# The first layer's start reordered: x first, modulation in two column halves

## The chip, the cores and the metric

One core of a Trainium2 chip runs the whole program in one launch. The metric is device time in microseconds (us), lower is better. TensorE (PE) multiplies and transposes, ScalarE (ACT), VectorE (DVE) and GpSimd (POOL) work on tiles, SyncE (SP) issues nearly all DMAs, in the order of its queue.

## The reference

The input x has 512 rows of 1024 columns. The program is a first block of four layers (gated linear attention "gla", a spatial gating unit, an attention with forget gates, and gla again) and a second block of two layers with a context stream. Only the start of the first layer is touched by the change:

```
cond = silu(c)                               # 1 x 1024
mod = cond @ w_mod[0] + b_mod[0]             # w_mod[0]: 1024 x 3072
shift, scale, gate = split(mod, 3)
h = rms_norm(x, norm_pre_g[0]) * (1 + scale) + shift
q, k, v, z, a_low = split(h @ gla_w_in[0])   # then decay, attention in chunks, head norm
o = (rms_norm(o, g_head) * silu(z)) @ w_out
x = x + gate * rms_norm(o, norm_post_g[0])
```

Shift and scale are one value for each of the 1024 columns of h. A product h @ W sums over these columns, in eight pieces of 128 (k = 0 to 7).

## The kernel before

Products are made from split operands: the left side H and each weight are held as a high part (fp32r) and the rest (low), and three products (hi·hi, hi·lo, lo·hi) are summed in PSUM. `weights` loads a weight tile ("wr", 256 KB, 5 buffers), and `split` writes "wh" on ScalarE and "wl" on GpSimd or DVE in turn (L256, L257; 4 buffers each). Large tiles of one row block (4 KB per partition) share the ring "t4" of 28 buffers. PSUM has eight banks, four for "pp" (products) and four for "pa" (the rest).

`setup` loads the identity, columns of c, `b_mod` and `norm_pre_g`, and makes `cond`. Then it loads the first 2048 columns of `w_mod[0]` in 16 tiles of 128 x 1024 (eight k, for each the shift and the scale columns), with the four tiles of x in the middle of them (`load_x` after the eighth). Each tile is multiplied with `cond`, in four column groups of 256 (L164). DVE copies the sums, TensorE transposes them, and DVE adds the bias and forms the multiplier, so that `m` (16 values for each of 128 partitions) holds the multiplier and the shift as columns (L166 to L183).

`first_block` begins with `prenorm`: x is normalized by row (`normed`: squares and a half on ScalarE, the rate on GpSimd, the other half on DVE), 32 transposes turn it (L501), and each transposed tile is read from PSUM with multiplier and shift (L507 on ScalarE, L509 on DVE) and split into H.hi and H.lo (L256, L257). All of this needs `m`. Then `gla` begins: the values of head 0 (`proj_tok`, K = 8, 256 columns, weights in four groups of two k; L310 to L312), `gla_decay` (L675 to L700), then q and k of head 0 (`proj_T`, L358 to L360), the attention, the gate z. The row `gh` (the head gains, broadcast over 128 partitions, 512 KB) is loaded as `gla` begins.

Generators yield at certain points; at each yield the driver takes 0.6 of a step (MRATE) of the background queue, which computes the modulations of the later layers (`mods`, L389 to L393). After the first group of the values (ADV = 1) `consts` loads the constants of the later stages. The Tile framework's planner turns the written program into the order of each engine's queue: it goes by priority (the order of writing) and by a simulated timeline, so each engine's queue is fixed when the kernel is built, and it need not be the order of writing.

Of the kernel before, what the change touches and what calls it, by code (L numbers as in the profile page):

```python
# [21 lines left out]
D = 1024  # L22
# [54 lines left out]
class Core:  # L77
    def __init__(self, ctx, tc, A):
        self.ctx, self.tc, self.nc, self.A = ctx, tc, tc.nc, A
        pool = lambda name, bufs, **k: ctx.enter_context(tc.tile_pool(name=name, bufs=bufs, **k))  # L80
        self.cp = pool("const", 1)
        self.wp = pool("w", 3)
        self.mx = pool("mx", 2)
        self.sm = pool("sm", 4)
        self.dp = pool("dram", 1, space=DRAM)
        self.ps = pool("ps", 1, space=PSUM)
        self.turn = {}
        self.n = 0
        self.ph, self.nlo = "", {}
        self.bg, self.rate, self.owed = {"m": [], "c": []}, {"m": MRATE, "c": 0}, {"m": 0, "c": 0}  # L90
        self.two = "c_2" in A
        self.share = False
        self.sk = ""

# [44 lines left out]
    def setup(self):  # L139
# [13 lines left out]
        w = [self.t("t4", [128, D]) for _ in range(16)]  # L153
        for i, x in enumerate(w):
            k, v = i // 2, i % 2
            nc.sync.dma_start(x, A["w_mod"][0][k * 128:(k + 1) * 128, v * D:(v + 1) * D])
            if i == 7:
                self.load_x()
        pad = self.cond["c"]
        ps = [self.psA() for _ in range(2)]  # L160
        for i, x in enumerate(w):
            k, v = i // 2, i % 2
            for g in range(4):
                nc.tensor.matmul(ps[v][g * 32:(g + 1) * 32, :256], pad[:, k, :], x[:, g * 256:(g + 1) * 256],  # L164
                                 start=(k == 0), stop=(k == 7))
        m = self.small("mcol", [128, 16], bufs=3)  # L166
        bias = self.col("b_mod0", 16)
        for v in (1, 0):
            sb = self.t("t1", [128, 256])
            nc.vector.tensor_copy(sb, ps[v][:, :256])  # L170
            pt = self.psA()
            for h in range(2):
                nc.tensor.transpose(pt[:, h * 128:(h + 1) * 128], sb[:, h * 128:(h + 1) * 128], self.ident)

            col = pt[:, :256].rearrange("p (h g r) -> p g h r", h=2, r=32)[:, :, :, 0]
            o = m[:, 8 - 8 * v:16 - 8 * v].rearrange("p (g h) -> p g h", h=2)
            bv = bias[:, v * 8:v * 8 + 8].rearrange("p (g h) -> p g h", h=2)
            nc.vector.tensor_tensor(o, col, bv, op=ALU.add)
            if v:
                pre = self.small("pre0", [128, 8], bufs=1)  # L180
                nc.vector.tensor_scalar(pre, self.col("pre0", 8), 32.0, None, ALU.mult)
                nc.vector.scalar_tensor_tensor(m[:, 0:8], m[:, 0:8], 1.0, pre, ALU.add, ALU.mult)
        self.m0 = m  # L183
# [104 lines left out]
    def proj_tok(self, H, nt, W, K, c0, n, out, r0=0, each=None, inturn=False, lead=1, wide="pp"):  # L288
# [42 lines left out]
        for g in groups:  # L331
            ws = [(k0, nk, self.weights(W, r0 + k0, nk, c0, n)) for k0, nk in g]
# [295 lines left out]
    def gla(self, H, j, O):  # L628
        nc, A = self.nc, self.A
        W = A["gla_w_in"][j]  # L630
        gh = self.bcast(A["gla_g_head"][j].rearrange("h d -> (h d)"), 1024, "t4")
        nc.vector.tensor_scalar(gh, gh, 0.5, None, ALU.mult)
# [9 lines left out]
        for h in range(4):  # L642
            v = []
            if h == 0:

                yield from values(h, v)
                yield from self.gla_decay(H, j, b)
            o = []
# [1523 lines left out]
    def first_block(self, dst=None):  # L2172
        A, x = self.A, self.x
        H, step = self.prenorm(x, 4, self.m0)
        for t, xn in enumerate([self.normed(x(t)) for t in range(4)]):
            step(t, xn)
        if ADV == 0:
            self.consts()
        yield
        for i in range(4):  # L2180
# [3 lines left out]
            if i % 3 == 0:  # L2184
                gen = self.phase("gla", self.gla(H, i // 3, O))
                if i == 0 and ADV:

                    for _ in range(ADV):
                        next(gen)
                        yield  # L2190
# [32 lines left out]
ADV = 1  # L2223
# [69 lines left out]
```

## Time and profile before

| | us |
|---|---|
| median of 3 runs | 3268.89 |
| lowest and highest run | 3267.01, 3275.14 |
| the profiled execution's own time | 3273.38 |
| its span | 3271.6 |
| TensorE busy in it | 3099.9 |
| DVE, ScalarE, GpSimd busy in it | 1691.7, 1458.9, 1306.4 |

The median is the time that a change is judged by. The profile is of one execution; its times begin at the span's start. An engine's busy time is what its instructions took, so what is missing to the span is idle time. A DMA share of 1.00 means that all 16 DMA engines are busy. Matmul records overlap (the array is pipelined), so the distance between two starts is the cost of one, not its printed duration. The clock column is the TensorE clock that was granted: 1.00 is 2.4 GHz, 0.50 is 1.2 GHz, and values between are means over a stretch that has both.

### The profile page before, as it was taken

What the parts mean: (1) busy time and instruction counts of PE and PEld (TensorE: products, weight loads), DVE (VectorE), ACT (ScalarE), POOL (GpSimd) and SP (SyncE); (2) the same over time, 40 slices, a digit from 0 to 9 for tenths busy, and PEclk for the clock granted to TensorE, in tenths of its full rate; (3) what the DMA queues carried; (4) which work ended last, traced back from release to release, by engine and by line L of the source; (5) the groups of instructions that cost most, each with busy time, mean ns of one, the idle gap of its engine ahead of it and who ended that gap; (6) DMA issues with size and microseconds to landing.
All of it is one profiled execution on the core that took longest, in us unless ns stands there. A gap on an engine that the chain in (4) does not pass through costs nothing.

```text
span 3271.6 us, 61127 instructions
## 1 busy us (share of the span) xinstructions
PE 3099.9 (95%) x23487; PEld 2650.2 (81%) x23487; DVE 1691.7 (52%) x3554; ACT 1458.9 (45%) x3173; POOL 1306.4 (40%) x1312
## 2 busy tenths in 40 slices
PE   7999999999999999989999999899999989999998
PEld 4878889878877778878887789898888877888887
DVE  2744564454555564666897757651112468641112
ACT  3424544354544543345544544453323447643323
POOL 2544453232212345344543113554445341154445
PEclk9999999999989999999999999999999999999999
DMA  7355645754435625354564335353333330043332
GB/s 239 91 152 171 212 132 165 235 164 133 134 117 169 191 76 150 113 160 128 164 171 130 109 86 144 114 160 94 100 123 110 109 90 2 24 142 97 97 123 90
DMA packets 477420, 426.25 MB, mean 130 GB/s; under 512 B 108038, under 2 KB 421609, under 8 KB 477129
## 3 DMA queue, kind: packets, MB, share of 16 engines
q1 hardware_dynamic: 477129, 422.35, 43.0%
q8 instruction: 185, 3.03, 0.4%
q14 instruction: 106, 0.87, 0.1%
HBM read 383.66 MB, written 38.03 MB: 129 GB/s over the span
## 4 chain that ended last, share of the span: by engine, by line
PE 74%; DVE 10%; DMA 5%; ACT 4%; issue 3%; POOL 3%; SPq 1%; POOLq 0%; DVEq 0%; ACTq 0%
PE ffn.pp L359 6%; PE ffn.pp L358 6%; PE ffn.pp L360 6%; PE mods.pa L393 3%; PE out.pp L310 2%; PE out.pp L311 2%; PE out.pp L312 2%; PE ffn.pa L312 2%; PE ffn.pa L311 2%; PE ffn.pa L310 2%; DMA mods.wm<-in_w_mod_dram 2%; PE fox.pp L312 1%; PE fox.pp L311 1%; PE fox.pp L310 1%; PE sgu.pp L310 1%
## 5 line engine op out<-in xcount | busy, mean ns | idle before, releaser
L257 POOL TENSOR_TENSOR ffn.wl<-ffn.wr,ffn.wh 128x512 fp32r<-128x512 f32 x258 | 332.8, 1293 | 345.6 <-ACT ffn.wh L256 345.5
L256 ACT ACTIVATE ffn.wh<-ffn.wr 128x512 fp32r<-128x512 f32 x258 | 162.5, 631 | 348.3 <-PE ffn.pp L360 144.6
L358 PE MATMUL ffn.pp<-pre.t,ffn.wh 128*128 128x512 f32 x672 | 261.6, 389 | 0.0
L359 PE MATMUL ffn.pp<-pre.t,ffn.wl 128*128 128x512 f32 x672 | 261.4, 389 | 0.0
L360 PE MATMUL ffn.pp<-pre.t,ffn.wh 128*128 128x512 f32 x672 | 261.4, 389 | 0.0
L598 DVE SCALAR_TENSOR_TENSOR ffn.t<-ffn.t,ffn.pp 128x512 f32<-128x512 f32 (+1 forms) x66 | 39.4, 597 | 243.9 <-ACT ffn.t L597 243.9
L257 POOL TENSOR_TENSOR gla.wl<-gla.wr,gla.wh 128x512 fp32r<-128x512 f32 x66 | 86.9, 1317 | 162.1 <-ACT gla.wh L256 148.2
L310 PE MATMUL gla.pp<-gla.wh,pre.t 128*128 128x256 f32 x512 | 150.6, 294 | 0.8 <-ACT gla.t L651 0.4
L311 PE MATMUL gla.pp<-gla.wl,pre.t 128*128 128x256 f32 x512 | 149.9, 293 | 0.0
L312 PE MATMUL gla.pp<-gla.wh,pre.t 128*128 128x256 f32 x512 | 149.4, 293 | 0.5 <-DVE pre.t L257 0.4
L359 PEld LDWEIGHTS ffn.pp<-pre.t,ffn.wl 128*128 128x128 f32 x672 | 126.1, 188 | 26.3
L360 PEld LDWEIGHTS ffn.pp<-pre.t,ffn.wh 128*128 128x128 f32 x672 | 126.1, 188 | 26.1
L358 PEld LDWEIGHTS ffn.pp<-pre.t,ffn.wh 128*128 128x128 f32 x672 | 126.1, 188 | 26.0
L257 POOL TENSOR_TENSOR ffn.cwl<-ffn.cwr,ffn.cwh 128x512 fp32r<-128x512 f32 x44 | 60.8, 1382 | 213.8 <-ACT ffn.cwh L256 188.7
L393 PE MATMUL mods.pa<-mods.wm,cond_c 128*32 128x256 f32 x1408 | 122.5, 402 | 16.0 <-DMA mods.wm<-in_w_mod_dram 15.6
L1140 DVE SCALAR_TENSOR_TENSOR ffn.t<-ffn.t,ffn.pp 128x512 f32<-128x512 f32 (+1 forms) x66 | 39.4, 597 | 176.2 <-PE ffn.pp L360 175.5
L256 ACT ACTIVATE ffn.cwh<-ffn.cwr 128x512 fp32r<-128x512 f32 x132 | 82.9, 632 | 104.6 <-PE ffn.pp L360 39.6
L310 PE MATMUL sgu.pp<-sgu.wh,pre.t 128*128 128x256 f32 x384 | 112.6, 293 | 6.9 <-DVE gdnp.at L1267 6.0
L311 PE MATMUL ffn.pa<-ffn.wl,ffn.t 128*128 128x512 f32 x304 | 118.3, 389 | 0.0
L312 PE MATMUL ffn.pa<-ffn.wh,ffn.t 128*128 128x512 f32 x304 | 118.3, 389 | 0.0
L310 PE MATMUL ffn.pa<-ffn.wh,ffn.t 128*128 128x512 f32 x304 | 112.7, 389 | 0.0
L312 PE MATMUL sgu.pp<-sgu.wh,pre.t 128*128 128x256 f32 x384 | 110.8, 289 | 1.3 <-DVE pre.t L257 1.1
(823 smaller groups left out, 10719.7 us busy)
## 6 DMA issues: line engine op xcount, KB each, us to landing
mods.wm<-in_w_mod_dram SPq DMA_DIRECT2D x176, 512.0 KB
gla.wr<-in_gla_w_in_dram SPq DMA_DIRECT2D x96, 256.0 KB
ffn.wr<-in_w_ffn_gate_dram SPq DMA_DIRECT2D x88, 256.0 KB
ffn.wr<-in_w_ffn_up_dram SPq DMA_DIRECT2D x88, 256.0 KB
ffn.wr<-in_w_ffn_down_dram SPq DMA_DIRECT2D x88, 256.0 KB
fox.wr<-in_fox_w_in_dram SPq DMA_DIRECT2D x64, 256.0 KB
sgu.wr<-in_sgu_w_in_dram SPq DMA_DIRECT2D x48, 256.0 KB
out.res_x<-out.t SPq DMA_DIRECT2D x24, 512.0 KB
```

The source lines that it names most:

```text
L256: nc.scalar.activation(hi, src, AF.Copy)
L257: (lo_eng or nc.vector).tensor_tensor(lo, src, hi.bitcast(F32), op=ALU.subtract)
L310: nc.tensor.matmul(o, H.hi(kk, s), w[0][:, k], start=(kk == 0 and first), stop=False)
L311: nc.tensor.matmul(o, H.hi(kk, s), w[1][:, k], start=False, stop=False)
L312: nc.tensor.matmul(o, H.lo(kk, s), w[0][:, k], start=False, stop=(kk == K - 1 and last))
L358: nc.tensor.matmul(o, wh[:, k], H.hi(kk), start=(kk == 0), stop=False)
L359: nc.tensor.matmul(o, wl[:, k], H.hi(kk), start=False, stop=False)
L360: nc.tensor.matmul(o, wh[:, k], H.lo(kk), start=False, stop=(kk == K - 1))
L393: nc.tensor.matmul(ps[g * 32:(g + 1) * 32, :256], pad[:, j, :], ws[j][:, g * 256:(g + 1) * 256], start=(j == 0), stop=(j == 7))
L598: nc.vector.scalar_tensor_tensor(dst, dst, 1.0, z, ALU.add, ALU.mult)
L1140: nc.vector.scalar_tensor_tensor(f, sg, 0.5, o[1], ALU.mult, ALU.mult)
```

## The change

x is loaded before any of `w_mod[0]`. Its rows are normalized and transposed without modulation, into four tiles `xT` in SBUF. The shift and scale columns come by halves: `half(i)` loads, for each k, columns i*512 to i*512 + 511 of both shift and scale in one tile [128, 2, 512]. `mods0` multiplies such tiles with `cond`, `mods1` makes four multiplier columns and four shift columns of it, and `norm0(H, i)` makes H's pieces k = 4i to 4i + 3 from `xT`: the high part directly on ScalarE, the full value on DVE, the low part on GpSimd (even k) or DVE (odd k).

The written order is: x, half 0 of the weights, normalization, six of eight k of half 0, transposes, the last two k, columns; then two weight tiles of the first head's values (`early`, k = 0 to 3), then the loads of half 1. In `first_block`: `norm0` of half 0, the first group of the values (k = 0, 1), half 1's k = 0 to 3, the second group (k = 2, 3), half 1's k = 4 to 7, columns, `norm0` of half 1, one yield, `consts`, the rest of `gla`. `gh` is loaded after the decay of head 0. The constant ADV is gone.

```diff
--- before.py
+++ after.py
@@ -91,6 +91,7 @@
         self.two = "c_2" in A
         self.share = False
         self.sk = ""
+        self.early = []
 
     def nm(self, s):
         self.n += 1
@@ -150,37 +151,76 @@
         self.columns("cols0", [("c", r(A["c"]), 8), ("b_mod0", r(A["b_mod"][0:1, 0:2 * D]), 16),
                                ("pre0", r(A["norm_pre_g"][0:1]), 8)])
         self.condition("c", ("c",))
-        w = [self.t("t4", [128, D]) for _ in range(16)]
-        for i, x in enumerate(w):
-            k, v = i // 2, i % 2
-            nc.sync.dma_start(x, A["w_mod"][0][k * 128:(k + 1) * 128, v * D:(v + 1) * D])
-            if i == 7:
-                self.load_x()
-        pad = self.cond["c"]
-        ps = [self.psA() for _ in range(2)]
-        for i, x in enumerate(w):
-            k, v = i // 2, i % 2
+        self.load_x()
+        src = A["w_mod"][0][:, 0:2 * D].rearrange("(k p) (v n) -> k p v n", p=128, v=2)
+
+        def half(i):
+            w = [self.t("t4", [128, 2, 512]) for _ in range(8)]
+            for k in range(8):
+                nc.sync.dma_start(w[k], src[k][:, :, i * 512:(i + 1) * 512])
+            return w
+
+
+        w = half(0)
+        self.m0 = self.small("mcol", [128, 16], bufs=3)
+        self.pre0 = self.small("pre0", [128, 8], bufs=1)
+        nc.vector.tensor_scalar(self.pre0, self.col("pre0", 8), 32.0, None, ALU.mult)
+        xn = [self.normed(self.x(t)) for t in range(4)]
+        ps = self.psA()
+        self.mods0(ps, w, 0, 6)
+        self.xT = [self.t("t4", [128, 2, 512]) for _ in range(4)]
+        for k in range(8):
+            pt = self.psP()
+            for t in range(4):
+                nc.tensor.transpose(pt[:, t * 128:(t + 1) * 128], xn[t][:, k * 128:(k + 1) * 128], self.ident)
+            (nc.vector.tensor_copy if k % 2 else nc.scalar.copy)(self.xT[k // 2][:, k % 2], pt)
+        self.mods0(ps, w, 6, 8)
+        self.mods1(ps, 0)
+        W = A["gla_w_in"][0]
+        old, self.ph = self.ph, "gla"
+        self.early = [self.weights(W, k0, 2, 1024, 256) for k0 in (0, 2)]
+        self.ph = old
+        self.w0 = half(1)
+
+    def mods0(self, ps, w, k0, k1):
+
+        for k in range(k0, k1):
             for g in range(4):
-                nc.tensor.matmul(ps[v][g * 32:(g + 1) * 32, :256], pad[:, k, :], x[:, g * 256:(g + 1) * 256],
-                                 start=(k == 0), stop=(k == 7))
-        m = self.small("mcol", [128, 16], bufs=3)
+                self.nc.tensor.matmul(ps[g * 32:(g + 1) * 32, :256], self.cond["c"][:, k, :],
+                                      w[k][:, g // 2, g % 2 * 256:g % 2 * 256 + 256], start=(k == 0), stop=(k == 7))
+
+    def mods1(self, ps, i):
+
+        nc, m = self.nc, self.m0
+        sb = self.t("t1", [128, 256])
+        nc.vector.tensor_copy(sb, ps[:, :256])
+        pt = self.psA()
+        for h in range(2):
+            nc.tensor.transpose(pt[:, h * 128:(h + 1) * 128], sb[:, h * 128:(h + 1) * 128], self.ident)
+
+        col = pt[:, :256].rearrange("p (h g r) -> p g h r", h=2, r=32)[:, :, :, 0]
         bias = self.col("b_mod0", 16)
         for v in (1, 0):
-            sb = self.t("t1", [128, 256])
-            nc.vector.tensor_copy(sb, ps[v][:, :256])
-            pt = self.psA()
-            for h in range(2):
-                nc.tensor.transpose(pt[:, h * 128:(h + 1) * 128], sb[:, h * 128:(h + 1) * 128], self.ident)
-
-            col = pt[:, :256].rearrange("p (h g r) -> p g h r", h=2, r=32)[:, :, :, 0]
-            o = m[:, 8 - 8 * v:16 - 8 * v].rearrange("p (g h) -> p g h", h=2)
-            bv = bias[:, v * 8:v * 8 + 8].rearrange("p (g h) -> p g h", h=2)
-            nc.vector.tensor_tensor(o, col, bv, op=ALU.add)
-            if v:
-                pre = self.small("pre0", [128, 8], bufs=1)
-                nc.vector.tensor_scalar(pre, self.col("pre0", 8), 32.0, None, ALU.mult)
-                nc.vector.scalar_tensor_tensor(m[:, 0:8], m[:, 0:8], 1.0, pre, ALU.add, ALU.mult)
-        self.m0 = m
+            c = 8 - 8 * v + 4 * i
+            bv = bias[:, v * 8 + 4 * i:v * 8 + 4 * i + 4].rearrange("p (g h) -> p g h", h=2)
+            nc.vector.tensor_tensor(m[:, c:c + 4].rearrange("p (g h) -> p g h", h=2), col[:, 2 * v:2 * v + 2], bv, op=ALU.add)
+        s = slice(4 * i, 4 * i + 4)
+        nc.vector.scalar_tensor_tensor(m[:, s], m[:, s], 1.0, self.pre0[:, s], ALU.add, ALU.mult)
+
+    def norm0(self, H, i):
+
+        nc, m = self.nc, self.m0
+        old, self.ph = self.ph, "pre"
+        for k in range(4 * i, 4 * i + 4):
+            if k % 2 == 0:
+                for part in (H.h, H.l):
+                    part[k // 2] = self.t("t4", (128, 2, 512), F32R)
+            x, a, b = self.xT[k // 2][:, k % 2], m[:, k:k + 1], m[:, 8 + k:9 + k]
+            hf = self.t("t2", [128, 512])
+            nc.scalar.activation(H.hi(k), x, AF.Identity, bias=b, scale=a)
+            nc.vector.tensor_scalar(hf, x, a, b, ALU.mult, ALU.add)
+            (nc.vector if k % 2 else nc.gpsimd).tensor_tensor(H.lo(k), hf, H.hi(k).bitcast(F32), op=ALU.subtract)
+        self.ph = old
 
     def setup2(self):
         nc, A = self.nc, self.A
@@ -329,7 +369,7 @@
 
             groups = groups[:-2] + [ks[-2:]]
         for g in groups:
-            ws = [(k0, nk, self.weights(W, r0 + k0, nk, c0, n)) for k0, nk in g]
+            ws = [(k0, nk, self.early.pop(0) if self.early else self.weights(W, r0 + k0, nk, c0, n)) for k0, nk in g]
             for t in range(nt):
 
                 for k0, nk, w in ws:
@@ -628,8 +668,6 @@
     def gla(self, H, j, O):
         nc, A = self.nc, self.A
         W = A["gla_w_in"][j]
-        gh = self.bcast(A["gla_g_head"][j].rearrange("h d -> (h d)"), 1024, "t4")
-        nc.vector.tensor_scalar(gh, gh, 0.5, None, ALU.mult)
         b = []
 
         def values(h, v):
@@ -645,6 +683,8 @@
 
                 yield from values(h, v)
                 yield from self.gla_decay(H, j, b)
+                gh = self.bcast(A["gla_g_head"][j].rearrange("h d -> (h d)"), 1024, "t4")
+                nc.vector.tensor_scalar(gh, gh, 0.5, None, ALU.mult)
             o = []
             yield from self.proj_T(H, 512, W, 8, [h * 128, 512 + h * 128], o)
             qT, kT = self.t("t2", [128, 512]), self.t("t2", [128, 512])
@@ -2171,23 +2211,23 @@
 
     def first_block(self, dst=None):
         A, x = self.A, self.x
-        H, step = self.prenorm(x, 4, self.m0)
-        for t, xn in enumerate([self.normed(x(t)) for t in range(4)]):
-            step(t, xn)
-        if ADV == 0:
-            self.consts()
-        yield
+        H = Split([None] * 4, [None] * 4, 2)
+        self.norm0(H, 0)
         for i in range(4):
             sc = self.scr["a", i]
             O = self.newO()
             self.context_rate(2 * i)
             if i % 3 == 0:
                 gen = self.phase("gla", self.gla(H, i // 3, O))
-                if i == 0 and ADV:
-
-                    for _ in range(ADV):
+                if i == 0:
+
+                    ps = self.psA()
+                    for k in (0, 4):
                         next(gen)
-                        yield
+                        self.mods0(ps, self.w0, k, k + 4)
+                    self.mods1(ps, 1)
+                    self.norm0(H, 1)
+                    yield
                     self.consts()
                 yield from gen
                 W = A["gla_w_out"][i // 3]
@@ -2220,7 +2260,6 @@
 LO = {'': 'p', 'pre': 'ppd', 'c': 'ddp', 'cgdnp': 'd', 'cmlap': 'd', 'gla': 'ppd', 'oddq': 'pdd', 'coddkv': 'pd', 'gdnp': 'ppd', 'oddkv': 'pdd', 'out': 'ddp', 'cout': 'pd', 'mlap': 'ppd', 'fox': 'pdd', 'cmla': 'd'}
 PREA = (3,)
 MRATE, MB = 0.6, 2
-ADV = 1
 PRI = 100
 DOWN = ((512, 512), (512, 256, 256))
 LEAD = (1, 1, 1, 1, 2)
```

## Rows read from the trace of the kernel before

**Rows 1.** The page: busy us of each engine, its share, instructions.

```profile
PE 3099.9 (95%) x23487; PEld 2650.2 (81%) x23487; DVE 1691.7 (52%) x3554; ACT 1458.9 (45%) x3173; POOL 1306.4 (40%) x1312
```

**Rows 2.** TensorE's stretches: length, busy, instructions, granted clock, DMA share, GB/s.

```profile
6.00:20.00 14.00, 8.65 (x64) 1.00 1.03 413
20.00:34.00 14.00, 9.16 (x67) 1.00 0.98 359
...
38.00:42.00 4.00, 0.65 (x6) 0.90 0.70 203
...
46.00:48.00 2.00, 2.00 (x11) 0.50 0.22 43
...
53.00:57.00 4.00, 1.70 (x12) 1.00 0.46 138
...
60.00:62.00 2.00, 2.00 (x14) 0.58 1.01 336
62.00:86.00 24.00, 24.00 (x118) 1.00 0.51 150
86.00:160.00 74.00, 71.26 (x530) 1.00 0.32 92
```

**Rows 3.** Timeline of TensorE, start of the run: start, us, engine, line.

```profile
6.49 2.25 PE L164 MATMUL .pa<-.t,cond_c 128*32 128x256 f32 x16 [2.75 <-DMA .t<-in_w_mod_dram]
...
10.21 1.08 PE L164 MATMUL .pa<-.t,cond_c 128*32 128x256 f32 x8 [0.20 <-DMA .t<-in_w_mod_dram]
11.49 1.08 PE L164 MATMUL .pa<-.t,cond_c 128*32 128x256 f32 x8 [0.20 <-DMA .t<-in_w_mod_dram]
...
31.86 1.08 PE L164 MATMUL .pa<-.t,cond_c 128*32 128x256 f32 x8 [0.24 <-DMA .t<-in_w_mod_dram]
...
34.40 4.01 PE L501 MATMUL pre.pa<-ident,.t 128*128 128x128 f32 x20
```

**Rows 4.** Timeline of TensorE, later.

```profile
60.51 1.08 PE L393 MATMUL mods.pa<-mods.wm,cond_c 128*32 128x256 f32 x8
...
62.76 0.28 PE L311 MATMUL gla.pp<-gla.wl,pre.t 128*128 128x256 f32 x1
62.88 0.28 PE L312 MATMUL gla.pp<-gla.wh,pre.t 128*128 128x256 f32 x1
...
68.65 0.64 PE L393 MATMUL mods.pa<-mods.wm,cond_c 128*32 128x256 f32 x8
```

**Rows 5.** Timeline of SyncE's DMA issues.

```profile
6.37 4.14 SPq L62 DMA_DIRECT2D .t<-in_x_dram  x4
...
21.70 0.39 SPq L279 DMA_DIRECT2D gla.wr<-in_gla_w_in_dram  x1
```

**Rows 6.** Timeline of ScalarE, DVE and GpSimd.

```profile
16.59 0.63 ACT L525 ACTIVATE .sq<-.t 128x512 f32<-128x512 f32 x1 [12.37 <-DMA .t<-in_x_dram]
...
23.98 0.49 DVE L530 TENSOR_SCALAR .t<-.t,.rr 128x512 f32<-128x512 f32 x1 [1.35 <-POOL .rr L539]
23.98 0.72 ACT L531 ACTIVATE .t<-.t,.rr 128x512 f32<-128x512 f32 x1 [0.41 <-POOL .rr L539]
...
33.27 1.27 POOL L257 TENSOR_TENSOR gla.wl<-gla.wr,gla.wh 128x512 fp32r<-128x512 f32 x1 [9.32 <-ACT gla.wh L256]
...
34.65 0.17 DVE L178 TENSOR_TENSOR .mcol<-.pa,cols 128x8 f32<-128x8 f32 x1
...
45.63 0.68 DVE L257 TENSOR_TENSOR pre.t<-pre.t,pre.t 128x512 fp32r<-128x512 f32 x1
...
45.72 1.72 POOL L257 TENSOR_TENSOR gla.wl<-gla.wr,gla.wh 128x512 fp32r<-128x512 f32 x1
```

**Rows 7.** DMA queue, 3130 to 3140 us: packets, MB, share of 16 engines.

```profile
q1 hardware_dynamic: 536, 0.97, 28.8%
```

**Rows 8.** TensorE's waits, whole run: us in total, times, longest.

```profile
PE pre.pa L501 <- DVE pre.t L530: 19.3, 8, 7.0
PE mods.pa L393 <- DMA mods.wm<-in_w_mod_dram: 15.6, 16, 2.7
```

## The prediction

> **What bounds the kernel now.** The page's table of engines comes first: TensorE is busy for 95% of the span, so a change pays only where it takes TensorE's idle or half-speed time away [rows 1]. Next, the table of stretches shows where that is at the start. From 6 to 34 us TensorE is busy 17.8 of 28 us while the DMA engines are full (share 1.03 and 0.98). From 38 to 42 us it works 0.65 of 4 us, from 46 to 48 us it runs at a granted clock of 0.50 (that is 1.2 GHz), and from 53 to 57 us it works 1.70 of 4 us. From 62 us on it is full: 24.00 of 24.00, then 71.26 of 74 [rows 2]. So whatever is gained before 62 us should arrive at the end, as long as the order of the later work stays as it is.
>
> The timeline of TensorE says what sits in those stretches [rows 3]. The multiplications of the condition with `w_mod[0]` (L164) go tile by tile at the pace of the landings, one group per 1.28 us, each group 1.08 us long; the last of 16 starts at 31.86. Then come the small transposes, and only at 34.40 the 32 transposes of the normalized x, 20 instructions in 4.01 us, 0.20 each. x itself was there long before: its issue starts at 6.37 [rows 5], ScalarE begins the squares at 16.59 and normalizes the last half tile at 23.98 [rows 6]. After that the shift and scale columns are ready at 34.82 (34.65 and 0.17) [rows 6]. The last product of the first head's values starts at 62.88 [rows 4]. That is my milestone: before, 63.2 us.
>
> One thing about the clock. A group of eight L164 instructions takes 1.08 us. The same shape in L393 takes 1.08 us at 60.51, in a stretch of granted clock 0.58, and 0.64 us at 68.65, where the clock is 1.00 [rows 2 to 4]. The stretches from 6 to 34 us print 1.00, but the duration is that of the slow group, and I go by the duration.
>
> **The change, part by part.** *Bytes.* x goes first: four tiles, first landing about 6.5 (the first L164 starts at 6.49), then one per 1.28 us, so 10.3 us [rows 3]. A half of the columns is again eight tiles of 512 KB, but in runs of 2 KB where the old tiles had 4 KB. A stretch of 10 us with almost nothing but 2 KB runs moved 0.97 MB in 28.8% of the engines' time, 337 GB/s [rows 7], against 413 / 1.03 = 401 GB/s at the start [rows 2]. That bounds a tile between 1.28 and 1.52 us; many of those transfers stood alone, so I take 1.40. Half 0 has landed at 10.3 + 11.2 = 21.5. The two early weight tiles (0.52 MB, runs of 1 KB, at 138 / 0.46 = 300 GB/s from the stretch 53 to 57 [rows 2]) take 1.75: 23.3. Half 1 lands at 34.5, with bounds of 32.0 and 36.6, where the last tile now lands just before 31.86. So the transfers end some 2.6 us later. Everything that SyncE's queue held behind `w_mod` (the remaining `gla.wr` tiles, constants, `mods.wm`) moves back by as much. The first `gla.wr`, issued at 21.70 now [rows 5], moves ahead of half 1. The 512 KB of `gh` leave this stage and its DVE multiplication with it, a gain I count at nothing.
>
> *TensorE until half 0 is done.* Eight groups of 1.08 = 8.6 us and 32 transposes of 0.20 = 6.4 us, from the first landed tile at 11.7. The normalized x is ready by 6.5 + 8.1 = 14.6 (16.59 to 24.70 now [rows 6]). If the transposes all stood in the 0.3 us gaps the work would end at 22.6; if they only add, at 26.7, which I take, since the gaps hold 2.5 us at most. The transposes' PSUM tiles are copied by ScalarE and DVE, eight copies of 128x512, near the 0.72 us of ScalarE's half tile at 23.98 [rows 6]; both engines have nothing else then. If that cover is gone, four copies on each engine cost 2.9 us.
>
> *Columns and modulation of half 0.* From the end of the last L164 group at 32.94 to 34.82 now: 1.9 us, so 28.6. Then ScalarE writes the high part and GpSimd the low part, 1.27 us for a 128x512 subtraction [rows 6], and 0.63 for ScalarE as in L525's pieces: 30.5.
>
> *The overlapped part.* TensorE then has half 1's groups, 8.6 us, and the products of k = 0 to 3. There are 4 (k) x 4 (row tiles) x 3 = 48 of them; at 62.76 and 62.88 they start 0.12 us apart [rows 4], 5.8 us, or twice that at half clock. Half 1's groups fill the hole between 28.6 and 30.5, so 28.6 + 8.6 + 5.8 = 43.0. Bounds: 35.6 (the last landing and one group) and 48.7 (half clock throughout).
>
> *After it.* Columns and modulation of half 1 again cost 1.9 + 1.9 = 3.8 us, in which TensorE has no product of the second half: 46.8. The planner can put products of k = 0 to 3 of the decay or of the first head's q there, once their weights have landed; I count half the hole, 1.9 us, as filled. The other 48 products are 5.8 us, and one L393 group with two small transposes, which stand before 62.88 now too, 1.7 us. That gives 46.8 - 1.9 + 5.8 + 1.7 = 52.4 against 63.2: a gain of 10.8 us.
>
> *A new collision.* The modulation's `tensor_scalar` now reads SBUF, where L509 read PSUM, and stands beside GpSimd's subtractions of the same half. The subtraction at 33.27 took 1.27 us with DVE at rest, that at 45.72, with DVE's two-input subtraction beside it since 45.63, 1.72 us [rows 6]. I charge 0.45 us for each of the two GpSimd subtractions of half 1, 0.9 us. The Trainium skill ("SBUF — State Buffer", section "Who interferes with whom") says that DVE and GpSimd share one port pair as a lock held for a whole instruction, and that `tensor_scalar` between SBUF tiles takes it too. The row at 45.72 agrees for the two-input form. By that rule all four `tensor_scalar` of half 1, at the 0.49 us of the one at 23.98 [rows 6], could hold GpSimd up in turn: 2.0 us in place of 0.9, and 3260 in place of 3259.
>
> *Steps of the background.* Two yields fewer reach the background queue in the first layer; at 0.6 of a step each that is one L393 group of 0.64 to 1.08 us done later, in a stretch where TensorE is full: nothing.
>
> Sum: 10.8 - 0.9 = 9.9 us. The profiled execution took 3273.4 us (span 3271.6), so 3263.5 by its count; it was 4.5 us above the median of 3268.9, from which the forecast is 3259. What a run of this kernel can tell from no change is about 0.3%, 9.8 us: the forecast lies on that line.
>
> **Rivals.**
>
> *The overlap fails.* The planner lays TensorE's queue out beforehand, and the engine takes it in order. If half 1's groups stand ahead of the products of half 0, each of which waits for a landing as L164 does now, the products begin at 34.5 + 1.1 = 35.6 and the columns of half 1 follow. Then only the 6.4 us of transposes have moved, less the 2.6 us of later landings: a gain of 4, 3265. For it: L164 stood so through 28 us without one of the transposes between. Against: the transposes then waited for columns and PSUM banks, and the new ones don't.
>
> *All overlaps.* Half 1's groups and the early products fit into the landings (35.6), and the products of k = 0 to 3 fill the hole: 35.6 + 1.9 + 5.8 + 1.7, some 45 to 47, a gain of 16 to 18; 3252. For it: TensorE was free for 4.84 us from 20 to 34 [rows 2]. Against: its half clock at the start.
>
> *Slower: the later order is redrawn.* The planner orders every instruction by a simulated timeline, so an earlier first layer may change which background group, transpose or weight tile stands ahead of what in the layers behind. The place is TensorE's waits for the pre-norm (L501 for DVE, 19.3 us in 8 waits) and for background weights (L393 for DMA, 15.6 us in 16) [rows 8]. It decides for slower when it adds 19.7 us, which is somewhat over half of these two; if they grew by two thirds, 23 us, the time would be 3282. For it: nothing fixes the order by hand. Against: the same instructions with the same waits follow, from a common shift.
>
> **How the numbers follow.** The forecast's case (gain of 6 to 14) has 0.46, the full overlap 0.15, the failed overlap 0.24, the redrawn order 0.15. About two thirds of the first lie above 9.8 us, so faster by over 0.3% is 0.30 + 0.15 = 0.45, within 0.3% 0.16 + 0.24 = 0.40, slower 0.15. The bounds of the place itself: a gain of 18 (3251) down to a loss of 3 with half clock in all products and a late half 1 (3272). A redrawn order goes both ways, so the range is 3246 to 3275, with some 0.06 below and 0.13 above. The likeliest case alone spans 3255 to 3263.
>
> **What would show it.** In the profile after: x's squares before 7 us; transposes in PSUM tiles of `pp` between 14 and 27 us; the first `gla.pp` products near 30 us and the last of the first head's values near 52; half 1's last landing between 32 and 37; TensorE full from about 51. The forecast is wrong in its sizes if the first products start after 35, and wrong in its reasoning if the milestone moves by 10 us and the total doesn't, or the total moves by more than the milestone: then the later order was redrawn.

## The result and the profile after

The changed kernel takes 3310.58 us (median of 4 runs, 3303.42 to 3316.66), beside 3271.41 us for the kernel before on the same chip: a ratio of 1.0117, 95% interval 1.0098 to 1.0136, some 38 us slower. The forecast was 3259 (3246 to 3275). The profiled execution took 3309.68 us, its span is 3307.9.

The page's table of engines, to be read beside [rows 1]:

```profile
PE 3122.5 (94%) x23487; PEld 2666.7 (81%) x23487; DVE 1694.5 (51%) x3551; ACT 1460.3 (44%) x3169; POOL 1303.1 (39%) x1308
```

TensorE has as many instructions as before, and their busy time is 22.6 us longer; the span grew by 36.3, so idle time grew by 13.7. More busy time for the same instructions goes with a lower clock: the mean granted clock of the profiled execution is 0.968, and 0.975 in the kernel before. A first layer that is a few us late explains neither.

TensorE's stretches, as in [rows 2] (length, busy, instructions, granted clock, DMA share, GB/s); the last row is a later stretch, in the fourth layer and behind it, that is needed further down:

```profile
6.00:20.00 14.00, 10.08 (x80) 1.00 1.00 374
20.00:34.00 14.00, 8.66 (x51) 0.69 0.70 181
38.00:42.00 4.00, 3.73 (x25) 0.64 1.05 388
...
53.00:57.00 4.00, 2.81 (x23) 1.00 0.78 219
57.00:60.00 3.00, 0.00 (x0) 0.93 0.05 11
62.00:86.00 24.00, 24.00 (x89) 0.84 0.37 113
86.00:160.00 74.00, 69.74 (x516) 0.95 0.38 111
...
1290.40:1597.90 307.50, 271.31 (x2538) 0.94 0.43 127
```

From 20 to 34 us the DMA engines are used at 0.70, where they were full before; from 57 to 60 TensorE does nothing (a small transpose, L268 in the timeline below, stands in its queue and waits 4.55 us for a constant to land); and from 62 to 86 it is full but at 0.84 of its clock, where [rows 2] has 1.00: 89 instructions in place of 118.

The timeline of TensorE, the parts that answer to [rows 3, 4] (L189 multiplies `w_mod[0]`, L175 transposes x, L199 turns the columns, L350 to L352 are the products of the values):

```profile
12.15 1.08 PE L189 MATMUL .pa<-.t,cond_c 128*32 128x256 f32 x8 [0.81 <-DMA .t<-in_w_mod_dram]
13.16 1.12 PE L175 MATMUL .pp<-ident,.t 128*128 128x128 f32 x4
14.21 1.08 PE L189 MATMUL .pa<-.t,cond_c 128*32 128x256 f32 x8
...
21.55 0.64 PE L189 MATMUL .pa<-.t,cond_c 128*32 128x256 f32 x8 [0.74 <-DMA .t<-in_w_mod_dram]
...
25.22 0.41 PE L350 MATMUL gla.pp<-gla.wh,pre.t 128*128 128x256 f32 x1 [2.05 <-ACT pre.t L220]
...
45.05 0.64 PE L189 MATMUL .pa<-.t,cond_c 128*32 128x256 f32 x8 [0.71 <-DMA .t<-in_w_mod_dram]
46.39 0.64 PE L189 MATMUL .pa<-.t,cond_c 128*32 128x256 f32 x8 [0.70 <-DMA .t<-in_w_mod_dram]
...
60.36 0.39 PE L268 MATMUL .pa<-ident,.t 95*128 95x95 f32 x1 [4.55 <-DMA .t<-in_gdn_conv_dram]
...
64.02 0.41 PE L352 MATMUL gla.pp<-gla.wh,pre.t 128*128 128x256 f32 x1
```

Half 0 went better than forecast: the transposes lie between the groups of L189, the last group of half 0 is at 21.55 and the first product at 25.22. Half 1 did not: its last group is at 46.39, waiting for its landing. The prediction's milestone, the last product of the first head's values, starts at 64.02, where it was at 62.88 before and 52.4 was forecast. The timeline of SyncE's issues, beside [rows 5], says why:

```profile
2.30 1.78 SPq L62 DMA_DIRECT2D .t<-in_x_dram  x4
4.12 7.47 SPq L160 DMA_DIRECT2D .t<-in_w_mod_dram  x8
12.03 2.04 SPq L319 DMA_DIRECT2D gla.wr<-in_gla_w_in_dram  x2
14.71 0.74 SPq L2181 DMA_DIRECT2D tri<-in_k_tri_dram  x1
16.07 0.34 SPq L1956 DMA_DIRECT2D dmask<-in_k_dmask_dram  x1
...
26.45 0.43 SPq L1978 DMA_DIRECT2D gqk<-in_gqa_k_norm_dram  x1
26.92 0.43 SPq L319 DMA_DIRECT2D gla.wr<-in_gla_w_in_dram  x1
27.40 0.47 SPq L429 DMA_DIRECT2D mods.wm<-in_w_mod_dram  x1
27.91 1.29 SPq L319 DMA_DIRECT2D gla.wr<-in_gla_w_in_dram  x2
29.25 7.12 SPq L160 DMA_DIRECT2D .t<-in_w_mod_dram  x8
```

The eight tiles of half 1 are issued from 29.25 on, where the forecast has them follow the two early weight tiles, at about 14. Small constants, three weight tiles and a tile of the background stand between. A constant takes some 0.3 us to issue, but the first ones come 1.36 us apart, close to the pace at which the 512 KB tiles of half 0 land. SyncE's waits from 14 to 23 us (us in total, times, longest) say that most of them wait for such a tile, L1963 (three of the constants) longest:

```profile
SPq L1963 <- DMA .t<-in_w_mod_dram: 3.0, 3, 1.0
```

So thirteen small constants held the queue for 12 us.

### The profile page after: what moved, and what is told of

It reads as the page before. It is cut to its first block, busy times and chain, and to the rows that moved or that the text cites. A ratio compares the mean times of both kernels' runs of the same rounds, so it can differ in the third digit from the quotient of the medians.

```text
span 3307.9 us, 61101 instructions
## 1 busy us (share of the span) xinstructions
PE 3122.5 (94%) x23487; PEld 2666.7 (81%) x23487; DVE 1694.5 (51%) x3551; ACT 1460.3 (44%) x3169; POOL 1303.1 (39%) x1308
## 4 chain that ended last, share of the span: by engine, by line
PE 42%; DVE 7%; POOL 2%; ACT 2%; issue 2%; DMA 1%; SPq 0%; DVEq 0%; POOLq 0%; ACTq 0%
PE ffn.pp L399 5%; PE ffn.pp L398 5%; PE ffn.pp L400 5%; PE ffn.pa L350 2%; PE ffn.pa L351 2%; PE ffn.pa L352 2%; PE odda.pa L1127 1%; PE odda.pa L936 1%; PE mla.pp L1746 1%; PE out.pp L350 1%; PE out.pp L352 1%; PE out.pp L351 1%; PE ffn.pp L351 1%; PE mla.pa L1127 1%; PE ffn.pp L350 1%
## 5 line engine op out<-in xcount | busy, mean ns | idle before, releaser
L350 PE MATMUL gla.pp<-gla.wh,pre.t 128*128 128x256 f32 x512 | 154.1, 301 | 7.2 <-ACT pre.t L220 3.3
L352 PE MATMUL gla.pp<-gla.wh,pre.t 128*128 128x256 f32 x512 | 152.3, 299 | 2.0 <-POOL pre.t L222 1.1
L433 PE MATMUL mods.pa<-mods.wm,cond_c 128*32 128x256 f32 x1408 | 133.0, 403 | 13.1 <-DMA mods.wm<-in_w_mod_dram 13.1
L352 PE MATMUL ffn.pa<-ffn.wh,ffn.t 128*128 128x512 f32 x304 | 118.3, 389 | 0.0
L350 PE MATMUL sgu.pp<-sgu.wh,pre.t 128*128 128x256 f32 x384 | 112.7, 294 | 3.3 <-DVE gdnp.at L1307 3.0
L352 PE MATMUL sgu.pp<-sgu.wh,pre.t 128*128 128x256 f32 x384 | 111.7, 291 | 1.9 <-DVE pre.t L297 1.2
L350 PEld LDWEIGHTS gla.pp<-gla.wh,pre.t 128*128 128x128 f32 x512 | 102.8, 201 | 12.9 <-ACT pre.t L220 3.8
```

The source lines that it names most:

```text
L350: nc.tensor.matmul(o, H.hi(kk, s), w[0][:, k], start=(kk == 0 and first), stop=False)
L352: nc.tensor.matmul(o, H.lo(kk, s), w[0][:, k], start=False, stop=(kk == K - 1 and last))
L433: nc.tensor.matmul(ps[g * 32:(g + 1) * 32, :256], pad[:, j, :], ws[j][:, g * 256:(g + 1) * 256], start=(j == 0), stop=(j == 7))
```

## The theories

A: two separate causes. Half 1 is issued late, because the planner gives the slots of the ring "t4" in the order of writing: half 1 is written behind `xT`, whose slots are taken only when the transposes run, and meanwhile the planner fills SyncE's queue with the constants. And the two missing yields move every later step of the background queue, so that the order of the later layers is another one. B: the late half alone is at fault, and all later differences follow from it. Other rivals came up on the way: that any earlier start redraws the later order, yields or not; that the weights of k = 4, late in their turn, are what keeps the gain back; that fewer background steps early simply cost, and more would give. The expectations name them by letters. The last three runs ask another question, and their letters stand for answers to it: is a shift at the start passed on to the end, as the prediction assumed, if the later order stays?

Where a total is compared below, it is the ratio times 3270 us, since each group of runs was timed beside its own runs of the kernel before, whose medians were 3266 to 3273 us. "First decay end" is the start of the first product of tile `glah.pa`, at 89.2 us before and 95.2 us after.

## The experiments

### Half 1 early

The early weights and half 1 are written directly behind half 0:

```diff
         w = half(0)
+        W = A["gla_w_in"][0]
+        old, self.ph = self.ph, "gla"
+        self.early = [self.weights(W, k0, 2, 1024, 256) for k0 in (0, 2)]
+        self.ph = old
+        self.w0 = half(1)
...
         self.mods1(ps, 0)
-        W = A["gla_w_in"][0]
-        old, self.ph = self.ph, "gla"
-        self.early = [self.weights(W, k0, 2, 1024, 256) for k0 in (0, 2)]
-        self.ph = old
-        self.w0 = half(1)
```

> The changed kernel, with the two early weight tiles and the eight loads of half 1 written right behind those of half 0, ahead of the normalization and the transposes. In the changed kernel half 1 was issued only from 29.25 us, behind fourteen small constants and three further weight tiles. Theory A (two causes: half 1 is issued late, and the two lost yields shift the background steps, so that later layers are laid out in another order): half 1 lands by 35 instead of 46 us, the first layer gains 10 to 14 us, the later loss of some 25 us stays: 3297 to 3301. Theory B (the late half is the whole loss, what is lost later follows from it): 3262 to 3272. Theory C (half clock and the engines' chains set the start, not the transfers): within 4 us of the changed kernel, 3306 to 3314.

Measured: 3301.16 us, ratio 1.0084 (1.0068 to 1.0100). The issue of half 1 moved from 29.25 to 14.41 and the first decay end from 95.2 to 88.6, so the place of writing is what made it late; the total came back by 11 us of 38. That the late half alone is at fault falls with this. Whether the slots of the ring made the difference, as theory A has it, or the place in the order of writing by itself, this edit does not separate.

### The two yields given back

```diff
                         self.mods0(ps, self.w0, k, k + 4)
+                        yield
```

> The changed kernel with one more yield behind each of the two first groups of the values, so that the background queue gets as many steps in the first layer as in the kernel before; half 1 stays late. Theory A: the order of the layers behind the first is nearly that of the kernel before, the some 25 us lost there come back, the 9 us of the first layer stay: 3280 to 3288. Theory B: as the changed kernel, 3306 to 3314. Theory D (any new order of the first layer throws the later order about, yields or not): anything from 3280 to 3320, with new places of loss.

Measured: 3287.60 us, ratio 1.0040 (1.0025 to 1.0055): 25 us back, with half 1 still late (first decay end 90.3). The yields are the larger part.

### Both

> Half 1 early and the two yields restored. Theory A: both losses are gone and the gain of the prediction's first layer is left: 3260 to 3270 against some 3271 of the kernel before. Theory B: the same as half 1 early alone. Theory C: the first layer keeps its loss, 3276 to 3284.

Measured: 3273.29 us (10 runs), ratio 1.0010 (0.9998 to 1.0023). 35 of the 38 us are back, close to the sum of the two; the gain that theory A expected to be left (3260 to 3270) is not there. What the first layer does now, first SyncE's issues of this kernel:

```profile
14.44 8.91 SPq L160 DMA_DIRECT2D .t<-in_w_mod_dram  x8
24.07 0.87 SPq L429 DMA_DIRECT2D mods.wm<-in_w_mod_dram  x1
25.45 0.99 SPq L2181 DMA_DIRECT2D tri<-in_k_tri_dram  x1
...
39.09 0.43 SPq L319 DMA_DIRECT2D gla.wr<-in_gla_w_in_dram  x1
```

Then its TensorE, timeline and stretches:

```profile
38.77 1.93 PE L189 MATMUL .pa<-.t,cond_c 128*32 128x256 f32 x32
41.26 0.44 PE L199 MATMUL .pa<-ident,.t 128*128 128x128 f32 x2 [0.55 <-DVE .t L196]
45.78 0.80 PE L350 MATMUL gla.pp<-gla.wh,pre.t 128*128 128x256 f32 x2 [4.09 <-ACT gla.wh L296]
```

```profile
41.00:46.00 5.00, 0.66 (x3) 0.96 0.98 266
46.00:53.00 7.00, 5.51 (x27) 0.54 0.58 146
53.00:57.00 4.00, 1.66 (x14) 1.00 0.09 25
```

Half 1 and the products of k = 0 to 3 are done by 40.7, better than the 43.0 of the forecast. But the weight tile for k = 4 stands behind the constants, is issued at 39.09, and TensorE waits 4.09 us for its high part; it then works from 46 to 53 at a clock of 0.54, near the lower of its two levels. The last product of the values starts at 59.8 us, at 62.9 in the kernel before; 52.4 was forecast for their end.

### The kernel before without its two yields

```diff
-        yield
         for i in range(4):
...
                         next(gen)
-                        yield
```

> The kernel before without the two yields of its first layer (the one behind the pre-norm and the one behind the first group of the values); nothing else is changed. Theory A: the start stays as it is, the later layers take the order of the changed kernel and lose 20 to 28 us: 3291 to 3299. Theory B: no change, 3267 to 3275. Theory D: a change of either sign, with other places of loss than in the changed kernel.

Measured: 3316.19 us, ratio 1.0123 (1.0101 to 1.0145). None of the change is in it, its first decay ends at 90.3, 1.1 us late, and it is as slow as the changed kernel; theory A had expected 20 to 28 us, and it is 40. So two yields are enough for a loss of this size (in the changed kernel the same two are worth 24 to 25 us, with half 1 early or late). In the traces, some 2660 of TensorE's 23487 instructions (compared by line and tile) stand at another place in its order than before. The loss lies far behind the place of the edit. By stages of TensorE, from the first product of one to that of the next (work of the stages around them runs in them too), the spatial gating unit is 13.1 us longer, the stage behind it ("gdnp") 8.7, the latent attention ("mla") 5.2, and "gdng" 15.2; from "ffn" on nothing is lost. In the first of these most of the loss can be placed. The table of stretches for the background's products alone, this kernel first and then the kernel before, has 14 groups of eight in place of 10 (34 groups are done ahead of it, 38 in the kernel before), and TensorE waits 9.6 us for their weights, 1.0 before:

```profile
341.10:429.70 88.60, 10.51 (x112) 0.90 0.63 195
```

```profile
341.00:416.50 75.50, 6.79 (x80) 1.00 0.62 195
```

Behind it, background work that comes late is no explanation: from there to "gdng", and in "gdng", the two kernels and the changed one have equally many of its instructions (896 and 128). TensorE in "gdng", from its first product to the first one of "ffn.pp", in this kernel, and then in the kernel before (after's row stands above):

```profile
1299.50:1610.10 310.60, 273.03 (x2537) 0.93 0.43 126
```

```profile
1269.80:1565.20 295.40, 267.00 (x2552) 0.95 0.45 131
```

Of the 15.2 us, 6.0 are busy time at a lower clock and 9.2 idle. In the changed kernel the same stage has 12.1 us more, 4.3 of them busy. TensorE's waits in this stretch of the changed kernel, those that grew:

```profile
PE gdng.pa L1094 <- DVE gdng.t L1623: 9.2, 2, 8.3
PE glah.pa L825 <- DVE glah.t L821: 3.0, 3, 1.8
PE gla.pp L350 <- ACT gla.t L691: 2.0, 2, 1.6
PE gla.pp L350 <- DVE gla.t L692: 1.8, 1, 1.8
```

The kernel before has 7.0, 0.7, 0.4 and none there, the kernel before without its yields 10.5, 2.6, 2.0 and 1.9. Together they grew by 7.9 and 8.9 us, nearly all of the idle time that the stretch gained in the two (7.8 and 9.2). The table of TensorE's waits of the changed kernel, whole run, beside [rows 8]:

```profile
PE pre.pa L541 <- DVE pre.t L570: 22.3, 7, 6.4
PE mods.pa L433 <- DMA mods.wm<-in_w_mod_dram: 13.1, 12, 3.8
```

The two waits that the prediction had named as the place moved by +3.0 and -2.5 us. In the kernel before without its yields the first is 19.2 and the second 23.7 us, 8.1 more. No single one carries the loss in both.

### Weights of k = 4 to 7 early too

As "both", with all four weight tiles of the values ahead of half 1:

```diff
-        self.early = [self.weights(W, k0, 2, 1024, 256) for k0 in (0, 2)]
+        self.early = [self.weights(W, k0, 2, 1024, 256) for k0 in (0, 2, 4, 6)]
```

> Half 1 early, the yields restored, and all four weight tiles of the first head's values (k = 0 to 7) loaded ahead of half 1. With both restored, TensorE still stood from 41.7 to 45.8 us for the weights of k = 4, which were issued at 39.09 behind fourteen small constants, and ran at half clock until 52. Theory E (what is left of the expected gain went to these late weights and the clock behind them): the last product of the first head's values moves from 60.0 to some 52 to 55 us, and the time to 3263 to 3268. Theory F (the gain of the start is given back later whatever the start does): the first layer ends earlier, the total stays within 4 us of 3273.

Measured: 3275.93 us, ratio 1.0031 (1.0020 to 1.0042). The wait of 4.09 us for the weights is gone. The last product of the values starts 7.8 us earlier than before:

```profile
55.06 0.28 PE L352 MATMUL gla.pp<-gla.wh,pre.t 128*128 128x256 f32 x1
```

The first decay ends at 83.0, 6.2 us earlier. The total is nevertheless 10 us above the kernel before: the stage of the forget-gate attention alone is 7.3 us longer, and "gdng" 3.7. An earlier first layer did not arrive at the end.

### More and fewer yields

The kernel before with three yields in place of one in the ADV loop; "weights early" with two yields in place of one behind each `mods0`; and the kernel before without the yield behind the pre-norm alone (the second cut is against the changed kernel, which has none there):

```diff
                         next(gen)
-                        yield
+                        for _ in range(3):
+                            yield
```

> The kernel before with two yields more behind the first group of the values, 1.2 background steps more instead of fewer. If fewer steps cost because work is left over (theory A1), the time is that of the kernel before or less, 3262 to 3273. If the kernel before stands at a good phase and any other phase costs (theory A2), it is slower: 3280 to 3310.

Measured: 3275.19 us, ratio 1.0025 (1.0012 to 1.0038).

```diff
                         self.mods0(ps, self.w0, k, k + 4)
+                        yield
+                        yield
```

> The version with four early weight tiles with two yields more than the kernel before has. Theory A1: as that version or better, 3260 to 3268. Theory A2: 15 to 40 us slower than it.

Measured: 3267.09 us, ratio 1.0006 (0.9994 to 1.0018), the first decay end at 83.8.

```diff
             self.consts()
-        yield
         for i in range(4):
```

> The kernel before without the yield behind its pre-norm alone, 0.6 of a background step less. Theory A1: about half of the 46 us that two yields cost, 3285 to 3300. Theory A2: no relation to the number of yields, somewhere from 3270 to 3315.

Measured: 3286.79 us, ratio 1.0054 (1.0036 to 1.0073). From the same kernel, one yield fewer costs 18 us, two fewer 40, two more 8. So fewer steps cost, as the theory of work left over (A1) expects, but it isn't simply that more background work early is better: every redrawn order tried here was at best as good as the one the kernel before has.

### A shift of the start with the order kept

Three copies of the kernel before load each `w_mod[0]` tile of the first layer as every other block of `c` columns, with c = 256, 128 and 64, so that the runs of its transfers are 1 KB, 512 B and 256 B in place of 4 KB. The columns of shift and scale are mixed by this; the work is the same.

```diff
-            nc.sync.dma_start(x, A["w_mod"][0][k * 128:(k + 1) * 128, v * D:(v + 1) * D])
+            nc.sync.dma_start(x.rearrange("p (a c) -> p a c", c=256), A["w_mod"][0][k * 128:(k + 1) * 128, 0:2 * D]
+                              .rearrange("p (a b c) -> p b a c", b=2, c=256)[:, v])
```

> The kernel before; each w_mod[0] tile of the first layer takes every other block of 256 columns, so that its runs are 1 KB instead of 4 KB (the columns of shift and scale are mixed, so h has other values). The bytes, the instructions and the order of every engine's queue are the same as before; only the landings are slower. At 300 GB/s (53 to 57 us of the kernel before, mostly 1 KB runs) a tile takes 1.75 us in place of 1.28, so the last of 16 lands some 7.5 us later (between 0 and 12). Theory A (the later order is what costs; with the same order a shift of the start is passed on one to one): the total is later by the shift of the first head's last value product, to within 3 us: some 3276 to 3278 where the kernel before has 3270. Rival B (later waits are for transfers and absorb a shift): under a third of the shift arrives, 3272 or less. Rival C (a shift alone already disturbs the later stages, through the clock and the waits): more than one and a half of the shift, over 3281.

> As the run with 1 KB runs, with blocks of 128 columns: runs of 512 B. Queues the same as before on every engine. The shift must be larger than with 1 KB, some 10 to 25 us. Theory A: the total is later by the shift of the first head's last value product, within 3 us. Rival B: under a third arrives. Rival C: more than one and a half of it arrives.

> As the two others, with blocks of 64 columns: runs of 256 B. Here the planner sees the slower transfers and draws another order (about 850 lines of TensorE's list differ, yields and background steps are the same in number). Theory A, that the redrawn order costs or gives a few us of its own in either direction: total minus shift is off zero by 3 us or more, while in the two runs with the same order it is within 3. Rival: only the number of background steps matters, an order redrawn by a shift alone costs nothing: total minus shift is within 3 us here too.

Measured: 3273.0 us, ratio 1.0008 (0.9994 to 1.0022); 3281.0 us, 1.0029 (1.0017 to 1.0041); 3294.89 us, 1.0068 (1.0054 to 1.0083). The last group of L164 on TensorE's timeline in the three, in this order, which [rows 3] have at 31.86:

```profile
35.45 1.08 PE L164 MATMUL .pa<-.t,cond_c 128*32 128x256 f32 x8 [0.42 <-DMA .t<-in_w_mod_dram]
```

```profile
39.96 1.08 PE L164 MATMUL .pa<-.t,cond_c 128*32 128x256 f32 x8 [0.70 <-DMA .t<-in_w_mod_dram]
```

```profile
48.74 1.08 PE L164 MATMUL .pa<-.t,cond_c 128*32 128x256 f32 x8 [1.20 <-DMA .t<-in_w_mod_dram]
```

The landings are 3.6 (where 7.5 was expected), 8.1 and 16.9 us later. In the first two, whose traces have the order of the kernel before on all engines (seven small products of "gdng" aside, which start within 0.1 us of one another), the shift of the first decay end and the change of the total agree (1.3 and 2.6, 8.4 and 9.5 us). With 1 KB runs both are inside the noise, so 512 B runs are the test: the total's interval is 5.6 to 13.4 us, and under a third of the shift, which rival B expects, lies outside it. In the third some 330 of TensorE's 23487 instructions stand at another place; it loses 22 us for a shift of 16.2, of which "gdng" alone has 7.9. Its rest of 6 us, 1.5 to 11 by the interval, is what a redrawn order costs there with the number of yields unchanged; the 3 us that were set as the line are not excluded.

### All runs side by side

| kernel | total, us | first decay end, us | rest, us | background groups by then |
|---|---|---|---|---|
| 1 KB runs, order kept | +2.6 | +1.3 | +1 | 5 |
| 512 B runs, order kept | +9.5 | +8.4 | +1 | 5 |
| 256 B runs | +22.2 | +16.2 | +6 | 5 |
| both | +3.3 | -0.1 | +3 | 5 |
| weights early, more yields | +2.0 | -5.4 | +7 | 7 |
| before, two yields more | +8.2 | -3.2 | +11 | 6 |
| the two yields given back | +13.1 | +1.1 | +12 | 6 |
| weights early | +10.1 | -6.2 | +16 | 5 |
| before, one yield less | +17.7 | -2.3 | +20 | 4 |
| half 1 early | +27.5 | -0.6 | +28 | 3 |
| the change | +38.3 | +6.0 | +32 | 2 |
| before, two yields less | +40.2 | +1.1 | +39 | 3 |

Total: (ratio - 1) x 3270, each uncertain by 4 to 7 us. The rest is total minus the shift at the first decay end. The last column has the background's groups (eight instructions of 0.64 to 1.08 us in all) that TensorE had done by then, 5 in the kernel before; the difference moves the second column by a few us. Where the order is kept, the rest is nothing beyond the noise. Where it is redrawn, it is 3 to 39 us, and the runs with 27 or more are those that lack both yields. Few groups done early go with a large rest (20 to 39 us with 2 to 4 of them), but the number does not settle it: with 5 it is 3 to 16 us among the redrawn orders.

## Why the prediction was wrong

The step that failed is "Steps of the background": "one L393 group of 0.64 to 1.08 us done later, in a stretch where TensorE is full: nothing". The work moved itself is small, as it says: by the first decay two groups more are undone without the yields in the kernel before, three in the changed kernel. The step left out that taking 1.2 steps less at the start moves the place of every later step in the planner's timeline. The two yields given back to the changed kernel return 25 of its 38 us; taken from the kernel before alone, they cost 40. The prediction's own sign, that "the total moves by more than the milestone", is what came: the milestone moved by 1.1 us, the total by 38. The third rival named this outcome, and gave it 0.15 and 3282, but with the earlier first layer as its cause and the waits for the pre-norm and the background weights as its place. The cause here was mostly the number of yields, which stands in the diff, and the place was spread over the stages, most of it up to "gdng", in waits and in the clock; of the waits it named, the first grew by 3.0 us in the changed kernel, and the second by 8.1 us only in the kernel before without yields.

The second wrong step is "Half 1 lands at 34.5". It was worked out as if SyncE issued the loads in the written order. (Its bounds, 32.0 and 36.6, come out of its own terms as 32.5 and 36.4; nothing hangs on it.) The pace was well sized: the groups of half 1 at 45.05 and 46.39 are 1.34 us apart, against 1.40 taken. Issued at 14.41, in the kernel with half 1 early, the transfers fill the DMA engines until about 34, as predicted; issued at 29.25 the last group starts at 46.39. The cost of the place was 11 us without the yields and 10 with them, each uncertain by some 7.

Of the smaller steps, the transposes went into the gaps: half 0 was done at 22.2, the lower of the two bounds (22.6, or 26.7, which was taken), and the first product started at 25.22, not 30.5. Columns and modulation of half 0 took 3.0 us from the last group's end to it, against 3.8 taken. That gain was lost again in two places that the sum lacked: at k = 4 the weights are late (4.09 us in "both"), since the remaining weight tiles stand behind the constants that SyncE has to issue; and the products run at the lower clock behind that wait (0.54 from 46 to 53), where the sum has 0.12 us apart. The prediction said that everything behind `w_mod` "moves back by as much" as 2.6 us, and didn't ask who waits for the weights among it. With the first mended ("weights early"; the clock from 46 to 53 is still 0.54), the milestone comes 7.8 us earlier where 10.8 was forecast, and the first decay ends 6.2 us earlier; even that did not reach the end.

The collision was priced at 0.45 us for each GpSimd subtraction of half 1. DVE and GpSimd of the changed kernel there; the second line is one of the four instructions of the first, and the last line has the shortest, middle and longest of all eight `tensor_scalar` (L221) of both halves in ns:

```profile
48.44 2.90 DVE L221 TENSOR_SCALAR pre.t<-.t,.mcol 128x512 f32<-128x512 f32 x4
49.36 1.53 DVE L221 TENSOR_SCALAR pre.t<-.t,.mcol 128x512 f32<-128x512 f32 x1
...
49.33 1.28 POOL L222 TENSOR_TENSOR pre.t<-pre.t,pre.t 128x512 fp32r<-128x512 f32 x1 [11.84 <-ACT pre.t L220]
...
51.73 1.36 POOL L222 TENSOR_TENSOR pre.t<-pre.t,pre.t 128x512 fp32r<-128x512 f32 x1 [1.12 <-ACT pre.t L220]
...
L221 DVE TENSOR_SCALAR pre.t<-.t,.mcol x8: 534/545/1532, 24.4 to 50.8; 128x512 f32<-128x512 f32 x8
```

The subtractions took 1.28 and 1.36 us, 0.1 in all above the undisturbed 1.27 of [rows 6]. Three of the four `tensor_scalar` of half 1 took 0.53 to 0.55 us; the one that started 0.03 us behind the first subtraction took 1.53 and ended 0.28 us after it, at 50.89. DVE lost about 1 us to it, and the second subtraction met none of the four. So the sum of 0.9 was about right, with the loser exchanged. The Trainium skill ("SBUF — State Buffer", section "Who interferes with whom") has the two engines share a port pair under an exclusive lock: whichever issues first keeps it for its whole instruction, and the other is blocked. This trace agrees, with GpSimd first by 0.03 us and DVE waiting 1 us; the 2.0 us on GpSimd that the prediction derived from that rule did not come.

What held is the assumption that was made with a condition: whatever shifts the start arrives at the end "as long as the order of the later work stays as it is". With 512 B runs it does, to within the noise (8.4 and 9.5 us). The change fails the condition.

What stays open is why an order is good or bad. The idle time of the changed kernel is spread over many waits, and the lower clock adds busy time in the same stages; which of the two comes first was not separated, and neither was the number of background steps from the order that it leads to. That none of the ten redrawn orders is better than that of the kernel before is an observation. No version tried beats the kernel before: "both" and "weights early, more yields" equal it.

## What to carry to other kernels

Where a planner lays out the queues from a simulated timeline, cost an edit in two parts: the shift it makes at its place, which arrived in full here where the queues behind kept their order, and the redrawing of everything behind, which here was worth up to 40 us and came mostly from a changed number of yields; compare the queues' order before trusting a sum, and keep the number of yields. A load need not be issued at its place in the written order: write early loads ahead of tiles that are written late, and put the weights that the next products need ahead of constants that nobody waits for.

## What the hardware showed beside

The time of a 512 KB tile by the length of its runs, as the distance between the last two groups that wait for a landing: 1.32 us with 4 KB ([rows 3] have 1.28 further ahead), 1.34 with 2 KB, 1.50 with 1 KB, 1.78 with 512 B, 2.28 with 256 B (2.41 further ahead). Below 2 KB the pace falls much less than the length: a sixteenth of the length, 256 B for 4 KB, costs a factor of 1.7 to 1.9.

The first group of L189 in the changed kernel takes 1.08 us, as at the lower clock, in a stretch that prints a clock of 1.00; from 15.81 to the end of half 0 a group takes 0.64 us, and at 40.01, where 0.50 is printed, 1.08 again. At the start of a run the printed clock says little; the duration of a known group says more.
